# Forget-gate codes of a gated linear attention as plain fp32 products on four groups of array columns

## The chip, the cores and the metric

One core of one Trainium2 chip runs the whole program. The metric is the device time of one execution in microseconds; the kernel before took 2001.63 us as the median of three runs (1999.76 to 2003.19).

## The reference, cut to what matters

A sequence of 256 tokens with 1024 features passes through four layers: two of a first kind (feed-forward, a mixer, feed-forward) and two of a second kind, which the change does not touch. The mixer of the first kind runs a neighbourhood attention and a gated linear attention (GLA) side by side. The change concerns how GLA's two forget gates, one for each direction, are made from the normed input:

```python
h = rmsnorm(x, mix_norm)
proj = h @ w_in                     # [256,1024] @ [1024,3104]
na_q, na_k, na_v, g_q, g_k, g_v, g_r, gf_code, gb_code = jnp.split(proj, offsets, axis=-1)
...                                 # gf_code, gb_code: 16 columns each
log_gf = jax.nn.log_sigmoid((gf_code @ w_gate_f + b_gate_f).astype(f32)) / GLA_TAU
log_gb = jax.nn.log_sigmoid((gb_code @ w_gate_b + b_gate_b).astype(f32)) / GLA_TAU
...                                 # w_gate: [16,256]
o_fwd = gla_chunked(qg, kg, vg, log_gf, True)
o_bwd = flip(gla_chunked(flip(qg), flip(kg), flip(vg), flip(log_gb), False))
gla_o = rmsnorm(o_fwd + o_bwd, gla_gain).astype(x.dtype)
gla_o = merge_heads(gla_o) * jax.nn.silu(g_r)
x = x + jnp.concatenate([na_o, gla_o], axis=-1) @ w_out
```

Everything is fp32.

## The kernel before, in words

Features lie on the 128 partitions and tokens in the free dimension: `x` is 128 x 8 x 256 (eight blocks `kt` of 128 features). Most products keep fp32 accuracy with three passes in a fast format, fp32r: each weight block of 128 x 128 is split into a high part `wh` (ScalarE, L320) and a low part `wl` (VectorE, L333), the activations into `Hh` and `Hl`, and `mm3` (L617 on) issues `wh*Hh` (L621), `wh*Hl` (L622) and `wl*Hh` (L623), 256 columns each. The norm's token factor `rs` is not known when the products start; it is multiplied in when a tile leaves PSUM.

All large weights of the program come as one stream (class `Stream`): chunks of 16 weight blocks, 1 MB each, are loaded by SyncE's DMA queue into four staging buffers `stg`, split in two halves on ScalarE and VectorE up to two chunks ahead (`next`, `fill`, `prep`), and taken block by block by the products (`block`). The layout functions on the host (`lay_mix1`) set the order of the blocks.

`mix1` (L795 on) is the mixer of the first kind, run once in each of two layers. `tiles` gives a PSUM tile of two blocks of 128 outputs (count=1: one block), with 24 matmuls a block. Two tiles of it make g_r; then one block makes the codes: its weight block is 128 columns wide, of which columns 0 to 15 hold the forward code, 32 to 47 the backward code and the rest are zeros. Two VectorE products (L827) scale the 16 rows of each into the tile `code`, whose other rows were set to 1 by GpSimd (L804). Row 16 of each direction so carries a 1 that multiplies the bias, which `lay_gate` put into row 16 of `wgate`. Then `gla_gates` (L897 on) is started as a generator: it advances by one step at each `tick`, which `tiles` calls after every fourth step of its loop over `kt`. Its first step is four plain fp32 products (L903: two directions, two halves of 128 outputs) over 32 rows of the array, `zp = wgate * code`; then come the absolute value, the exponential and the logarithm on ScalarE (L909 to L912), the minimum and maximum on VectorE (L910), the difference (L914) and the running sums (L919). Meanwhile TensorE makes two tiles of GLA's keys and queries, two of the attention's values, four of its queries and keys (each followed by a softmax pair, `na_pair`, L1047 on), GLA's values, and the output product `mixed_out` (L869 on).

The mixer's stream has 17*8 + 2*32 + 64 = 264 blocks (`MIX1_BLOCKS`). That is 16.5 chunks, padded to 17; `mixed_out` ends with `st.skip()`, which drops the padding. With the codes' eight blocks in the third chunk, all later chunk boundaries fall into the middle of a tile.

The program's text is not the order of issue. A planner of the framework places each engine's instructions when the kernel is built: among those whose inputs and buffers are ready by its own cost estimates it takes the one that is needed first. An instruction written later can so be issued earlier on its engine; each engine then runs its list in that fixed order. PSUM and SBUF buffers under one tag are reused in turn, and a new user waits for the release of the old one. The lines that matter here, beside those in the listing:

```python
def mm3(self, out, w, kt, start, stop, clear=True):
    h, l = w
    ...
    mm(out[:, :n], h, self.Hh[:, kt, :n], ...)   # L621
    mm(out[:, :S], h, self.Hl[:, kt], ...)       # L622
    return mm(out[:, :n], l, self.Hh[:, kt, :n], ...)  # L623
```

One other place already uses plain fp32 products on four groups of 32 array columns: `compress` (L1427), in the last layer, with 16 products of 128 columns each, group after group:

```python
g = m % 4
nc.tensor.matmul(p[32 * g:32 * g + 32, :P], Z[j][:, m], w[:, m * P:(m + 1) * P], start=m < 4, stop=m >= 12)
```

Of the kernel before, what the change touches and what calls it, by code (L numbers as in the profile page):

```python
# [9 lines left out]
F32 = mybir.dt.float32  # L10
# [7 lines left out]
P = 128  # L18
S = 256
# [53 lines left out]
def lay_mix1(w_in, w_out):  # L73

    q, k, v, gq, gk, gv, gr, gf, gb = np.split(w_in, np.cumsum([512, 512, 512, 256, 256, 512, 512, 16]), 1)
    code = np.zeros((D, P), w_in.dtype)
    code[:, 0:RANK] = gf
    code[:, 32:32 + RANK] = gb
    q, k, gq, gk, gr, code, gv, v = [blocks(m) for m in (q, k, gq, gk, gr, code, gv, v)]
    seq = [gr, code]  # L80
    for i in range(2):
        seq += [gq[:, i], gk[:, i]]
    seq += token_blocks(v)
    for i in range(4):
        seq += [q[:, i], k[:, i]]
    wo = blocks(w_out)
    seq += token_blocks(gv) + [wo[:, :, :4], wo[:, :, 4:]]
    return cat(seq)


MIX1_BLOCKS = 17 * 8 + 2 * 32 + 64


def lay_rpb(rpb):
# [9 lines left out]
    return np.ascontiguousarray(b.reshape(2, P, 4 * 2 * S))  # L104


def lay_gate(wf, bf, wb, bb):

    o = np.zeros((64, 256), wf.dtype)
    for at, w, b in ((0, wf, bf), (32, wb, bb)):  # L110
        o[at:at + RANK] = w
        o[at + RANK] = b
    return o


def gla_masks():
# [21 lines left out]
def layout(i):  # L138
    o = {}
    for l in range(DEPTH):  # L140
        o[f"a1_{l}"] = lay_ffn(i["ffn1_wg"][l], i["ffn1_wu"][l], i["ffn1_wd"][l])
    o["xT"] = np.ascontiguousarray(i["x"][0].T.reshape(KD, P, S).transpose(1, 0, 2))
    for l in range(DEPTH):
        o[f"m1_{l}"] = lay_mix1(i["w_in"][l], i["w_out"][l])
        o[f"nab_{l}"] = lay_rpb(i["na_rpb"][l])
        o[f"wgate_{l}"] = lay_gate(i["w_gate_f"][l], i["b_gate_f"][l], i["w_gate_b"][l], i["b_gate_b"][l])
        o[f"a2_{l}"] = lay_ffn(i["ffn2_wg"][l], i["ffn2_wu"][l], i["ffn2_wd"][l])
    parts = []
    for l in range(DEPTH):
        parts += [(f"f1n{l}", i["ffn1_norm"][l]), (f"mxn{l}", i["mix_norm"][l]), (f"f2n{l}", i["ffn2_norm"][l]),  # L150
                  (f"nag{l}", i["na_gain"][l]), (f"glg{l}", i["gla_gain"][l])]
    parts += [("fin1", i["final_norm"]), ("fin2", i["final_norm_g_2"])]
    for l in range(DEPTH):
        mw = np.ascontiguousarray(i["mod_w_2"][l].T)
        o[f"mw_{l}"] = np.ascontiguousarray(mw.reshape(36, 2, P, D).transpose(0, 2, 1, 3).reshape(36, P, 2 * D))
        parts += [(f"mb{l}", i["mod_b_2"][l])] + [(f"ng{l}{j}", i["norm_g_2"][l, j]) for j in range(3)]
        w1 = i["ffn_w1_2"][l]
        for j in range(2):
            o[f"b{j}_{l}"] = lay_ffn(w1[j][:, :FF], w1[j][:, FF:], i["ffn_w2_2"][l, j])
    parts += [("cw", i["lru_conv_w_2"][0].reshape(-1)), ("cb", i["lru_conv_b_2"][0]),  # L160
              ("bab", np.concatenate([i["lru_ba_2"][0].reshape(-1), i["lru_bx_2"][0].reshape(-1)])),
              ("lam", i["lru_lambda_2"][0])]
    o["cond"] = np.ascontiguousarray(np.broadcast_to(i["c_2"], (P, D)))
    o["m2a"] = lay_mix2a(i["mix0_in_w_2"][0], i["mix0_out_w_2"][0])
    o["lru"] = lay_lru(i["lru_wa_2"][0], i["lru_wx_2"][0])
    o["m2b"] = lay_mix2b(i["mix1_in_w_2"][0], i["mix1_out_w_2"][0])
    o["cw1"] = np.ascontiguousarray(i["cmp_w1_2"][0].reshape(2, 16, P, P).transpose(0, 2, 1, 3).reshape(2, P, 2048))
    o["cpos"] = np.ascontiguousarray(i["cmp_pos_2"][0].reshape(2, 16, P).transpose(2, 0, 1))
    w2 = i["cmp_w2_2"][0]
    o["cw2"] = np.ascontiguousarray(np.concatenate([w2[0], w2[0], w2[1]], 1))  # L170
    o["rope"] = rope_tables()
    o["rot"] = rotation()
    o["causal"] = np.where(np.arange(P)[None] > np.arange(P)[:, None], np.float32(-1e30), np.float32(0))
    o["cmask"] = cmp_mask()
    o["masks"] = gla_masks()
    o["cols"] = lay_cols(parts)
    o["ident"] = np.eye(P, dtype=np.float32)
    return o
# [201 lines left out]
class Kern:  # L380
# [414 lines left out]
    def mix1(self, st, l, then):  # L795
        nc = self.nc
        with self.tc.tile_pool(name="mx", bufs=1) as mp, self.tc.tile_pool(name="m2", bufs=2) as m2, \
                self.phase_psum():
            self.bank, self.nst, self.pp = 256, 4, "pp"
            self.mp, self.m2 = mp, m2  # L800
            sgr = mp.tile([P, GH, S], F32, name="sgr")
            code = mp.tile([64, S], F32, name="code")
            wgate = mp.tile([64, S], F32, name="wgate")
            nc.gpsimd.memset(code, 1.0)  # L804
            nc.sync.dma_start(wgate, self.a[f"wgate_{l}"])
            kq = mp.tile([P, 2, 2, S], F32, name="kq")
            vg = mp.tile([P, 2, 512], F32, name="vg")
            vn = mp.tile([P, 2, 512], F32, name="vn")
            self.na = mp.tile([P, 4, S], F32, name="na")
            self.mh = mp.tile([P, 4, S], F32R, name="mh")  # L810
            self.ml = mp.tile([P, 4, S], F32R, name="ml")

            def scaled(p, w):
                t = m2.tile([P, 2, S], F32, name="t", tag="e0")
                nc.vector.tensor_tensor(t, p, self.rs2(), op=OP.mult)
                nc.scalar.activation(w, t, AF.Silu)

            p0 = self.tiles(st, first=True)

            def mid():  # L820
                scaled(p0, sgr[:, 0:2])

            p = self.tiles(st, mid=mid)
            scaled(p, sgr[:, 2:4])
            p = self.tiles(st, count=1)
            for at in (0, 32):
                nc.vector.tensor_mul(code[at:at + RANK], p[at:at + RANK, 0], self.rs[at:at + RANK])  # L827
            gates = self.gla_gates(l, code, wgate)
            self.bg.append(gates)
            if l == DEPTH - 1:  # L830
                self.small()
            for i in range(2):
                p = self.tiles(st)
                nc.vector.scalar_tensor_tensor(kq[:, 1, i], p[:, 0], 0.125, self.rs, op0=OP.mult, op1=OP.mult)
                nc.vector.tensor_mul(kq[:, 0, i], p[:, 1], self.rs)
            while gates in self.bg:
                self.tick()
            at = self.mp.tile([P, GH, 4, P], F32, name="at")

            def gla():  # L840
                yield from self.gla_grams(kq, at)
                yield
                yield from self.gla_out(l, at, vg, sgr)

            self.have_vg = self.pairs = 0
            self.bg.append(gla())
            for n in range(2):
                self.token_major(st, vn, n, 4)
            self.sqn, self.normed = None, False
            for i in range(4):  # L850
                p = self.tiles(st, ticks=1)
                qk = m2.tile([P, 2, S], F32, name="qk", tag="qk")
                nc.vector.scalar_tensor_tensor(qk[:, 0], p[:, 0], 0.125, self.rs, op0=OP.mult, op1=OP.mult)
                nc.vector.tensor_mul(qk[:, 1], p[:, 1], self.rs)
                if i % 2 == 0:
                    bias = st.raws.pop(0)
                self.bg.append(self.na_pair(l, i, qk, vn, bias))
            self.bg.append(self.na_norm())
            for n in range(2):
                self.token_major(st, vg, n, 1)  # L860
                self.have_vg = n + 1
            self.norm_start(*then())
            mm = nc.tensor.matmul

            while not self.normed:
                self.tick()
            self.mixed_out(st, (self.mh, self.ml), (self.gh, self.gl_))
# [29 lines left out]
    def gla_gates(self, l, code, wgate):  # L897
# [2 lines left out]
        zp = [self.pd.tile([P, 2, S], F32, name="zp", tag="pd") for _ in range(2)]  # L900
        for d in range(2):
            for i in range(2):
                nc.tensor.matmul(zp[d][:, i], wgate[32 * d:32 * d + 32, i * P:(i + 1) * P], code[32 * d:32 * d + 32],  # L903
                                 start=True, stop=True)
        yield
        az = mp.tile([P, 2, 2, S], F32, name="az")
        G = mp.tile([P, 2, 2, S], F32, name="G")
        for d in range(2):
            nc.scalar.activation(az[:, d], zp[d], AF.Abs)  # L909
            nc.vector.tensor_scalar(G[:, d], zp[d], 0.0, -288.0, op0=OP.min, op1=OP.max)  # L910
        nc.scalar.activation(az, az, AF.Exp, scale=-1.0)
        nc.scalar.activation(az, az, AF.Ln, bias=1.0)  # L912
        yield
        nc.vector.tensor_sub(G, G, az)  # L914
        self.INC = mp.tile([P, 2, 2, S], F32, name="INC")
        self.VAL = mp.tile([P, 2, 2, S], F32, name="VAL")
        for d in range(2):
# [767 lines left out]
```

## Time and profile before

| | before |
|---|---|
| median of three runs | 2001.63 us (1999.76 to 2003.19) |
| the profiled execution's own time | 2000.05 us |
| its span, first to last instruction | 1998.3 us |
| PE busy | 1962.8 us (98%), 13164 matmuls |
| DVE busy | 1592.4 us (80%) |
| ACT busy | 1179.2 us (59%) |
| POOL busy | 181.0 us (9%) |
| loaded | 430.92 MB, 216 GB/s in the mean |
[...]

PE is TensorE's matmuls, PEld its weight loads, DVE VectorE, ACT ScalarE, POOL GpSimd, SP SyncE with its DMA queue. Times in rows are microseconds from the start of the span unless marked ns. A matmul's duration includes the way through the array, so consecutive matmuls overlap: what one costs is read from the distance between two starts. A plain fp32 matmul appears as two instructions. The mixer of the first kind runs from about 195 to 327 us and from about 694 to 825 us.

### The profile page before, as it was taken

Reading aid. Unit: us, or ns where it says so; the run is one execution under the profiler, and the core shown is the slowest. Engines: PE = TensorE matmul, PEld = TensorE weight load, DVE = VectorE, ACT = ScalarE, POOL = GpSimd, SP = SyncE. Lnnn points to the kernel's source line nnn. Section 1 sums busy time; section 2 is a strip of 40 time slices with the busy share of each in tenths; the row PEclk is TensorE's granted clock in tenths of the full one; section 3 lists DMA queues with packets and bytes.
Section 4 is the critical chain, followed back from the end, with each engine's and each line's share of the span. In section 5 each row is a group of like instructions: output and inputs, shape, how many; then the busy total and the mean of one; then the engine's idle time right before and its main releaser. Section 6 shows DMA issues by size and latency. Waiting matters only on the chain.

```text
span 1998.3 us, 33132 instructions
## 1 busy us (share of the span) xinstructions
PE 1962.8 (98%) x13164; PEld 1779.0 (89%) x13164; DVE 1592.4 (80%) x2554; ACT 1179.2 (59%) x1977; POOL 181.0 (9%) x201
## 2 busy tenths in 40 slices
PE   8999999999999999999999999999999999999998
PEld 7888989888988898988898889898899888889887
DVE  8987888987888688898789878898667667988663
ACT  6654566554555566655556546675546655877652
POOL 3001002000100100200110010120010001111001
PEclk9999999999999999999999999999999999999999
DMA  7976434887687643488658864377555556315551
GB/s 293 326 280 237 173 136 172 297 295 264 230 290 273 238 177 135 177 297 291 257 194 294 295 246 162 126 260 278 190 190 189 190 190 200 108 50 195 190 185 56
DMA packets 67883, 430.92 MB, mean 216 GB/s; under 512 B 11408, under 2 KB 14096, under 8 KB 16656
## 3 DMA queue, kind: packets, MB, share of 16 engines
q1 hardware_dynamic: 67440, 428.28, 59.3%
q8 instruction: 103, 1.69, 0.3%
q10 hardware_dynamic: 288, 0.52, 0.1%
q14 instruction: 52, 0.43, 0.1%
HBM read 427.73 MB, written 1.05 MB: 215 GB/s over the span
## 4 chain that ended last, share of the span: by engine, by line
PE 88%; DVE 7%; ACT 3%; DMA 1%; issue 1%; POOL 0%; DVEq 0%; SPq 0%; ACTq 0%
PE pp L605 25%; PE pd L605 16%; PE pp L606 13%; PE pd L606 8%; PE pp L621 5%; PE pp L623 5%; PE pp L622 5%; PE po L883 2%; DVE wl L333 2%; PE pt L1275 1%; DVE Hl L686 1%; ACT wh L320 1%; PE pv L671 1%; PE pv L672 1%; PE pv L673 1%
## 5 line engine op out<-in xcount | busy, mean ns | idle before, releaser
L333 DVE TENSOR_TENSOR wl<-stg,wh 128x1024 fp32r<-128x1024 f32 x646 | 787.1, 1245 | 110.2 <-PE pd L606 44.8
L320 ACT ACTIVATE wh<-stg 128x1024 fp32r<-128x1024 f32 x646 | 667.4, 1053 | 299.4 <-PE pp L605 100.1
L605 PE MATMUL pp<-H,wh 128*128 128x512 f32 x2176 | 755.0, 390 | 0.0
L606 PE MATMUL pp<-H,wl 128*128 128x256 f32 x2176 | 613.6, 282 | 0.0
L605 PE MATMUL pd<-act,wh 128*128 128x512 f32 x1408 | 488.5, 390 | 0.0
L605 PEld LDWEIGHTS pp<-H,wh 128*128 128x128 f32 x2176 | 408.4, 188 | 85.8 <-DVE t L614 0.5
L606 PEld LDWEIGHTS pp<-H,wl 128*128 128x128 f32 x2176 | 411.2, 189 | 0.0
L606 PE MATMUL pd<-act,wl 128*128 128x256 f32 x1408 | 397.1, 282 | 0.0
L621 PE MATMUL pp<-Hh,wh 128*128 128x256 f32 (+1 forms) x1192 | 343.3, 288 | 7.6 <-ACT wh L291 6.8
L623 PE MATMUL pp<-Hh,wl 128*128 128x256 f32 (+1 forms) x1192 | 336.3, 282 | 1.2 <-DVE wl L333 1.0
L622 PE MATMUL pp<-Hl,wh 128*128 128x256 f32 x1192 | 334.9, 281 | 1.8 <-DVE Hl L686 1.8
L605 PEld LDWEIGHTS pd<-act,wh 128*128 128x128 f32 x1408 | 264.3, 188 | 55.4
L606 PEld LDWEIGHTS pd<-act,wl 128*128 128x128 f32 x1408 | 266.1, 189 | 0.0
L621 PEld LDWEIGHTS pp<-Hh,wh 128*128 128x128 f32 x1192 | 224.8, 189 | 12.3 <-ACT wh L291 6.8
L622 PEld LDWEIGHTS pp<-Hl,wh 128*128 128x128 f32 x1192 | 226.2, 190 | 3.9 <-DVE Hl L686 2.6
L623 PEld LDWEIGHTS pp<-Hh,wl 128*128 128x128 f32 x1192 | 225.1, 189 | 2.2 <-DVE wl L333 1.4
L700 DVE SCALAR_TENSOR_TENSOR stg<-stg,cond 128x1024 f32<-128x1024 f32 x144 | 176.2, 1226 | 35.1 <-DMA stg<-mw 32.0
L682 ACT ACTIVATE act<-a 128x256 fp32r<-128x256 f32 x176 | 73.4, 417 | 141.8 <-DVE a L758 129.4
L522 POOL TENSOR_TENSOR acc<-sq 128x256 f32<-128x256 f32 x16 | 17.3, 1081 | 1174.2 <-ACT sq L518 1174.1
L683 DVE TENSOR_TENSOR act<-a,act 128x256 fp32r<-128x256 f32 x176 | 76.4, 434 | 44.0 <-ACT act L682 44.0
L522 POOL TENSOR_TENSOR acc<-acc,sq 128x256 f32<-128x256 f32 x87 | 79.6, 918 | 330.3 <-ACT sq L518 326.6
L745 ACT ACTIVATE s<-t 128x256 f32<-128x256 f32 x136 | 56.6, 416 | 83.8 <-DVE t L614 83.3
(311 smaller groups left out, 2098.2 us busy)
## 6 DMA issues: line engine op xcount, KB each, us to landing
stg<-b SPq DMA_DIRECT2D x132, 1024.0 KB, 4.8
stg<-a SPq DMA_DIRECT2D x129, 1024.0 KB, 4.8
stg<-mw SPq DMA_DIRECT2D x72, 1024.0 KB, 5.8
stg<-m SPq DMA_DIRECT2D x34, 1024.0 KB, 4.8
stg<-m2a SPq DMA_DIRECT2D x14, 1024.0 KB, 4.8
stg<-m2b SPq DMA_DIRECT2D x12, 1024.0 KB, 5.0
stg<-nab SPq DMA_DIRECT2D x4, 1024.0 KB, 4.9
cond<-cond SPq DMA_DIRECT2D x6, 512.0 KB, 4.6
```

The lines of the kernel that those rows point to most:

```text
L320: self.k.nc.scalar.activation(h[:, sl], self.raw[c][:, sl], AF.Copy)
L333: self.k.nc.vector.tensor_sub(l[:, sl], t[:, sl], f(h[:, sl]))
L522: nc.gpsimd.tensor_tensor(s2, acc, sq, op=OP.add)
L605: mm(p, h, parts, start=start, stop=False)
L606: return mm(p[:, :S], l, parts[:, 1], start=False, stop=stop)
L621: mm(out[:, :n], h, self.Hh[:, kt, :n], start=start and clear, stop=False, skip_group_check=not clear)
L622: mm(out[:, :S], h, self.Hl[:, kt], start=False, stop=False, skip_group_check=not clear)
L623: return mm(out[:, :n], l, self.Hh[:, kt, :n], start=False, stop=stop, skip_group_check=not clear)
L682: nc.scalar.activation(hi, src, AF.Copy)
L683: nc.vector.tensor_sub(lo, src, f(hi))
L700: self.nc.vector.scalar_tensor_tensor(sl, sl, 1.0, self.cond, op0=OP.mult, op1=OP.mult, accum_out=self.mod[l][:, 2 * c + g:2 * c + g + 1])
L745: nc.scalar.activation(s, t[:, 0], AF.Silu)
```

## The change

The codes leave the weight stream. The 32 code columns come as a tensor of their own (`code_l`, 128 x 8 x 32, 128 KB), loaded at the start of the mixer and multiplied once by the norm's gain on VectorE. The products are plain fp32 on the unnormed, unsplit `x`: block `kt` goes to the group of 32 array columns `kt % 4`, so that four partial sums of the 32 code rows stand on the 128 partitions of one PSUM tile, each over two blocks. One VectorE product by `rs` takes all 128 rows into `code`. The gate weights are repeated four times along the 128 rows (`lay_gate`, 256 KB), with zeros for the other direction's rows, so that the gate products over 128 rows add the partial sums. The bias moves into ScalarE's and VectorE's instructions, which therefore work on one half of 128 outputs at a time; the lower limit moves into the difference. The stream has 256 blocks, which is 16 whole chunks.

```diff
 def lay_mix1(w_in, w_out):
-    code = np.zeros((D, P), w_in.dtype)
-    code[:, 0:RANK] = gf
-    code[:, 32:32 + RANK] = gb
-    q, k, gq, gk, gr, code, gv, v = [blocks(m) for m in (q, k, gq, gk, gr, code, gv, v)]
-    seq = [gr, code]
+    code = np.concatenate([gf, gb], 1).reshape(KD, P, 2 * RANK).transpose(1, 0, 2)
+    q, k, gq, gk, gr, gv, v = [blocks(m) for m in (q, k, gq, gk, gr, gv, v)]
+    seq = [gr]
...
-    return cat(seq)
-MIX1_BLOCKS = 17 * 8 + 2 * 32 + 64
+    return cat(seq), np.ascontiguousarray(code).reshape(P, -1)
+MIX1_BLOCKS = 16 * 8 + 2 * 32 + 64
...
-def lay_gate(wf, bf, wb, bb):
-    o = np.zeros((64, 256), wf.dtype)
-    for at, w, b in ((0, wf, bf), (32, wb, bb)):
-        o[at:at + RANK] = w
-        o[at + RANK] = b
-    return o
+def lay_gate(wf, wb):
+    o = np.zeros((4, 2 * RANK, 2, 256), wf.dtype)
+    o[:, :RANK, 0] = wf
+    o[:, RANK:, 1] = wb
+    return o.reshape(P, 512)
...
@@ mix1
-            code = mp.tile([64, S], F32, name="code")
-            wgate = mp.tile([64, S], F32, name="wgate")
-            nc.gpsimd.memset(code, 1.0)
-            nc.sync.dma_start(wgate, self.a[f"wgate_{l}"])
+            code = mp.tile([P, S], F32, name="code")
+            wgate = mp.tile([P, 2, S], F32, name="wgate")
+            nc.sync.dma_start(wgate, self.a[f"wgate_{l}"].rearrange("p (d n) -> p d n", d=2))
+            wcode = mp.tile([P, KD, 2 * RANK], F32, name="wcode")
+            nc.sync.dma_start(wcode, self.a[f"code_{l}"].rearrange("p (k n) -> p k n", k=KD))
...
-            p = self.tiles(st, count=1)
-            for at in (0, 32):
-                nc.vector.tensor_mul(code[at:at + RANK], p[at:at + RANK, 0], self.rs[at:at + RANK])
+            nc.vector.tensor_mul(wcode, wcode, self.g.unsqueeze(2).to_broadcast([P, KD, 2 * RANK]))
+            p = self.ps.tile([P, 2, S], F32, name="pco", tag="pp")
+            for kt in range(KD):
+                r = slice(32 * (kt % 4), 32 * (kt % 4) + 32)
+                nc.tensor.matmul(p[r, 0], wcode[:, kt], self.x[:, kt], start=kt < 4, stop=kt >= 4)
+            nc.vector.tensor_mul(code, p[:, 0], self.rs)
+            self.tick()
...
@@ gla_gates
-                nc.tensor.matmul(zp[d][:, i], wgate[32 * d:32 * d + 32, i * P:(i + 1) * P], code[32 * d:32 * d + 32],
-                                 start=True, stop=True)
+                nc.tensor.matmul(zp[d][:, i], wgate[:, d, i * P:(i + 1) * P], code, start=True, stop=True)
...
-            nc.scalar.activation(az[:, d], zp[d], AF.Abs)
-            nc.vector.tensor_scalar(G[:, d], zp[d], 0.0, -288.0, op0=OP.min, op1=OP.max)
+            for i in range(2):
+                b = self.col(f"bgate{l}", 2 * d + i)
+                nc.scalar.activation(az[:, d, i], zp[d][:, i], AF.Abs, bias=b)
+                nc.vector.tensor_scalar(G[:, d, i], zp[d][:, i], b, 0.0, op0=OP.add, op1=OP.min)
...
-        nc.vector.tensor_sub(G, G, az)
+        nc.vector.scalar_tensor_tensor(G, G, -288.0, az, op0=OP.max, op1=OP.subtract)
```

The host also adds the four bias columns of each layer to the small table `cols`.

## Rows read from the trace of the kernel before

**Rows 1.** The page's chain that ended last: share of the span by engine.

```profile
PE 88%; DVE 7%; ACT 3%; DMA 1%; issue 1%; POOL 0%; DVEq 0%; SPq 0%; ACTq 0%
```

**Rows 2.** Busy us (x instructions) by stretch: PE, PEld, DVE, ACT, POOL; clock, DMA, GB/s.

```profile
225.00:285.00 60.00, 56.81 (x496) 51.05 (x495) 56.28 (x98) 36.06 (x73) 0.87 (x1) 1.00 0.45 160
724.00:784.00 60.00, 57.07 (x497) 51.16 (x497) 56.22 (x98) 36.43 (x73) 0.87 (x1) 1.00 0.45 163
```

**Rows 3.** Waits of PE, 195 to 335 us: us in total, times, longest.

```profile
PE pav L1089 <- ACT pt L1082: 1.9, 1, 1.9
PE pss L1054 <- DVE qk L854: 0.9, 2, 0.7
PE pp L622 <- DVE Hl L686: 0.5, 1, 0.5
```

**Rows 4.** Timeline of PE around the codes, layer 0: start, duration, engine, line, operation.

```profile
207.38 0.28 PE L621 MATMUL pp<-Hh,wh 128*128 128x256 f32 x1
...
210.21 0.28 PE L621 MATMUL pp<-Hh,wh 128*128 128x256 f32 x1
...
211.51 0.28 PE L623 MATMUL pp<-Hh,wl 128*128 128x256 f32 x1
211.72 1.14 PE L903 MATMUL zp<-code,wgate 32*128 32x256 f32 x8
212.79 0.38 PE L621 MATMUL pp<-Hh,wh 128*128 128x256 f32 x1
213.01 0.28 PE L622 MATMUL pp<-Hl,wh 128*128 128x256 f32 x1
```

**Rows 5.** Timeline of `compress`: plain fp32 on four column groups, and what follows.

```profile
1689.31 0.84 PEld L1427 LDWEIGHTS pq<-stg,Z 128*32 128x32 f32 x32 [0.96 <-issue]
1689.34 1.08 PE L1427 MATMUL pq<-stg,Z 128*32 128x128 f32 x32 [0.78 <-issue]
...
1690.35 0.39 PE L621 MATMUL pp<-Hh,wh 128*128 128x258 f32 x1
...
1690.57 0.28 PE L622 MATMUL pp<-Hl,wh 128*128 128x256 f32 x1
```

**Rows 6.** All of line L1427: durations in ns, minimum/median/maximum.

```profile
L1427 PEld LDWEIGHTS pq<-stg,Z x64: 106/110/110, 1689.3 to 1694.0; 128*32 128x32 f32 x64
```

**Rows 7.** Timeline of PE: plain fp32 over 128 rows and 128 columns (L1212).

```profile
1221.23 1.02 PE L1212 MATMUL pl<-xc,wlru 128*128 128x256 f32 x4
...
1222.21 0.28 PE L622 MATMUL pp<-Hl,wh 128*128 128x256 f32 x1
```

**Rows 8.** Timeline of DVE around the codes, layer 0.

```profile
207.58 0.69 DVE L815 TENSOR_TENSOR t<-pp,rs 128x512 f32<-128x512 f32 x1 [1.72 <-PE pp L623]
208.19 2.35 DVE L333 TENSOR_TENSOR wl<-stg,wh 128x1024 fp32r<-128x1024 f32 x2
210.48 0.86 DVE L827 TENSOR_TENSOR code<-pp,rs 16x256 f32<-16x256 f32 x2
213.51 1.29 DVE L910 TENSOR_SCALAR G<-zp 128x512 f32<-128x512 f32 x2 [2.18 <-ACT az L909]
```

**Rows 9.** Timeline of DVE in layer 1: the first and last of 27 small ones (`small`, written after the codes).

```profile
697.93 0.16 DVE L433 TENSOR_SCALAR sp<-lam 128x4 f32<-128x4 f32 x1
...
706.52 0.17 DVE L436 TENSOR_SCALAR ns<-ns 128x4 f32<-128x4 f32 x1
```

**Rows 10.** The page's DVE group that splits weights, and its DMA issues.

```profile
L333 DVE TENSOR_TENSOR wl<-stg,wh 128x1024 fp32r<-128x1024 f32 x646 | 787.1, 1245 | 110.2 <-PE pd L606 44.8
...
stg<-m SPq DMA_DIRECT2D x34, 1024.0 KB, 4.8
```

**Rows 11.** Issue of the table of masks on SyncE, and median landing of a 256 KB load.

```profile
196.12 0.58 SPq L926 DMA_DIRECT2D masks<-masks  x1
...
rope<-rope SPq DMA_DIRECT2D x2, 256.0 KB, 3.6
```

**Rows 12.** Timeline of ACT at the gates' first step, layer 0.

```profile
212.88 1.08 ACT L909 ACTIVATE az<-zp 128x512 f32<-128x512 f32 x2 [2.85 <-PE zp L903]
```

More of the change, by code (lines that the diff above doesn't have):

```diff
@@ L143, in layout @@
     for l in range(DEPTH):
-        o[f"m1_{l}"] = lay_mix1(i["w_in"][l], i["w_out"][l])
+        o[f"m1_{l}"], o[f"code_{l}"] = lay_mix1(i["w_in"][l], i["w_out"][l])
         o[f"nab_{l}"] = lay_rpb(i["na_rpb"][l])
-        o[f"wgate_{l}"] = lay_gate(i["w_gate_f"][l], i["b_gate_f"][l], i["w_gate_b"][l], i["b_gate_b"][l])
+        o[f"wgate_{l}"] = lay_gate(i["w_gate_f"][l], i["w_gate_b"][l])
         o[f"a2_{l}"] = lay_ffn(i["ffn2_wg"][l], i["ffn2_wu"][l], i["ffn2_wd"][l])
@@ L150, in layout @@
         parts += [(f"f1n{l}", i["ffn1_norm"][l]), (f"mxn{l}", i["mix_norm"][l]), (f"f2n{l}", i["ffn2_norm"][l]),
-                  (f"nag{l}", i["na_gain"][l]), (f"glg{l}", i["gla_gain"][l])]
+                  (f"nag{l}", i["na_gain"][l]), (f"glg{l}", i["gla_gain"][l]),
+                  (f"bgate{l}", np.concatenate([i["b_gate_f"][l], i["b_gate_b"][l]]))]
     parts += [("fin1", i["final_norm"]), ("fin2", i["final_norm_g_2"])]
```

## The prediction

> **What bounds the kernel now.** I read the page first. Its chain of waits lies on TensorE for 88% of the span and on VectorE for 7% [rows 1], so a change is worth what it takes off TensorE's list, unless TensorE stands waiting where the change works. The busy times by stretch say where it does: in the 60 us of each mixer that hold the attention's softmax and GLA's gram products, VectorE is busy for 56.28 and 56.22 us and TensorE for only 56.81 and 57.07 [rows 2]. So the mixer has two regimes: around the codes (205 to 225 us) TensorE runs without a gap, and from 225 to 285 us VectorE's list sets the pace and TensorE loses about 3 us. The waits name the places: 1.9 us for the transposed softmax weights, 0.9 us for an eviction of queries and keys, 0.5 us for the low part of the normed input at the mixer's end [rows 3]. Last I read the timelines around the codes for the prices.
>
> **The change part by part, for one layer; there are two.**
>
> *The codes' products leave the three-pass stream.* Their 24 matmuls run from 207.38 us to the start of the next tile at 210.21 us: 2.83 us, 0.118 us each [rows 4]. All of it is TensorE's own time, with nothing beside it that has to wait: minus 2.83 us.
>
> *Plain fp32 products on four column groups come in.* Eight products are 16 instructions of 256 columns, 4096 columns in all. The nearest rows are those of `compress`, which has the same form on the same four groups: 32 instructions of 128 columns, also 4096. They go from 1689.34 us to the next start at 1690.35 us, 1.01 us, and the matmul after that start takes 0.22 us to its successor instead of 0.12, so 0.10 us more [rows 5]. What the switch into a tiled array costs shows at the gate products, which start 0.21 us after the matmul before them instead of 0.12: 0.09 us [rows 4]. I take 1.01 + 0.10 + 0.09 = 1.20 us. Below it stands perfect concurrency: plain fp32 over the full array costs 0.215 us per instruction of 256 columns (four of them from 1221.23 us to 1222.21 less one step of 0.12, so 0.86 us [rows 7]), and four to a group make 0.86 us. Above it stands no concurrency, 16 x 0.215 + 0.19 = 3.63 us. I take the middle value because the row has the same form, and only the columns per instruction differ.
>
> *The weight loads of the small blocks.* There are 16, of 32 columns. In `compress` 32 such loads last about 0.110 us each [rows 6], 3.5 us one after another, and yet all lie within 0.84 us [rows 5]; they overlap, and 1.20 us holds them. [...]
>
> *The gate products go from 32 rows to 128.* Before, two directions stand on two row groups and partly overlap: from 211.63 us (211.51 plus a step) to 212.89 us (213.01 less a step), 1.26 us with both switches [rows 4]. After, eight instructions use the whole array: 8 x 0.215 = 1.72 us [rows 7]. Plus 0.46 us; the two ends, 0.36 and 0.56, differ only by whether a switch remains.
>
> TensorE's sum: -2.83 + 1.20 + 0.46 = -1.17 us per layer, -2.34 us for both.
>
> *The code weights times the gain, on VectorE.* This is new: 256 columns on 128 partitions, at 0.43 us as the code evictions (0.86 us for two of 256 columns [rows 8]). Its inputs are early: the table of masks, written far behind, is issued at 196.12 us, and 256 KB take 3.6 us to land [rows 11], so both new loads are there by about 201 us. The codes start at 207.38 us. VectorE sits idle for 1.72 us before 207.58 us [rows 8], and in layer 1 the planner put 27 small instructions, written after the codes, into just such gaps from 697.93 us on [rows 9]. So I cost it at nothing. If the planner puts it where it is written, it stands behind the eviction of g_r's second tile (207.58 + 0.69 us), ends at 208.70 us, and TensorE waits 1.2 us from 207.50; that is the second rival.
>
> *The code eviction* is one instruction instead of two (minus 0.43 us of VectorE). Behind it in the list come the low halves of the next chunk (2.35 us [rows 8]), needed only after a whole tile, 16 x 3 x 0.118 = 5.7 us later. The gate products come twelve matmuls, 1.41 us, after the code products; an eviction of 0.43 us fits, and behind one half split (1.2 us) it would be late by 0.2 us. I cost that at nothing.
>
> *The gates' first step in quarters.* VectorE's two minima of 512 columns (1.29 us [rows 8]) become four of 256, at 0.43 us 1.72: plus 0.43 us. ScalarE's two absolute values (1.08 us [rows 12]) become four, between 1.08 and 2.16 us. Neither is on TensorE's path; TensorE reaches the gate products 1.63 us earlier and leaves them 1.17 us earlier, so the gates' chain begins earlier by as much as TensorE does, and the VectorE-bound stretch moves with it.
>
> *One chunk less in the stream.* 34 loads of 1 MB become 32 [rows 10]; two halves of the low split go, 2 x 1.245 = 2.49 us of VectorE per layer [rows 10], and two of the high split on ScalarE. New loads of 0.38 MB take the place of 0.064 MB. DMA is busy for 0.45 of the stretch [rows 2], so the bytes count nothing. VectorE's net is -2.49 + 0.43 - 0.43 + 0.43 = -2.06 us. Where TensorE is the bound this is worth nothing. In the VectorE-bound stretch it is worth something, but only half a chunk falls there: each boundary moves from the middle of a tile to its start, so a low half is due half a tile later, 1.25 us of VectorE less before the attention's end, against a TensorE loss of 3.19 us (60 - 56.81 [rows 2]). Bounds: all TensorE waits but the eviction's go (-1.8 us, the 1.9 us of the pair less a remnant), or the splits now fall on the softmax (third rival). I take -0.4 us, a third of 1.25, since the waits hang on latencies more than on the sum: -0.8 us for both layers.
>
> **Sum.** -2.34 - 0.8 = -3.1 us. The profiled execution took 2000.05 us around a span of 1998.3 us; it would take 1996.9 us. It lies 1.58 us under the median of the runs, 2001.63 us; so I forecast 1998.5 us.
>
> **Rivals.**
>
> First, *VectorE's relief is cashed in full.* For it: the 3 us lost per layer [rows 2, 3], and 2.06 us less work. Against: the wait of 1.9 us ends on a chain of softmax, transpose and copy that the change does not shorten. Then -2.34 - 2 x 1.8 = -5.9 us: 1995.7 us.
>
> Second, *the small weights are scaled too late.* For it: the text has the scaling behind the eviction. Against: [rows 9]. Two waits of 1.25 us: -2.34 + 2.5 = +0.2 us: 2001.8 us.
>
> Third, on the other side, *the splits land on the softmax.* With boundaries at tile starts, the next chunk's splits ask for VectorE just when a tile's eviction and its softmax pair do, and TensorE waits for a low half. The place is the four tiles of queries and keys; the price one half, 1.245 us, each: 4 x 1.245 - 1.17 = +3.8 us per layer, 2009.2 us. It makes the kernel slower than 0.2% from three of the four boundaries on. For it: VectorE is busy for 94% there [rows 2]. Against: splits run up to two chunks ahead, and no row of the waits names `wl` [rows 3].
>
> Fourth, *the small loads are paid one after another*: 16 x 0.110 + 0.86 + 0.19 = 2.81 us instead of 1.20, so +0.44 us per layer: 2002.5 us. [...] Against: [rows 5].
>
> Fifth, *the four groups do not overlap*, so the change does not do what it says: 3.63 us, +1.26 us per layer: 2004.2 us.
>
> **How the numbers follow.** The forecast has 0.55, with a range of its own from 1996.0 to 2001.0 us; the rivals in order 0.22, 0.08, 0.09, 0.04, 0.02. Two tenths of a per cent, 4.0 us, is about what a measurement of this kernel can tell from no change: faster is below 1997.6 us, slower above 2005.6 us. The forecast gives 0.15 to faster, the first rival 0.20: 0.35. Slower takes 0.09 of the third and 0.01 of others: 0.10. The rest, 0.55, is same. The range 1993.5 to 2004.5 us reaches over all but the third rival.
>
> **What would show it.** The distance from the last matmul of g_r's second tile to the first of the next tile should be about 1.3 us instead of 2.83 + 0.12; with a gap before the small products, the second rival holds; with more than 2.5 us and no gap, the fourth or fifth. The gate products should take 1.72 us. `stg<-m` should count 32, L333's group 642. In the stretch with the softmax, TensorE's waits for `pt`, `qk` and any new one for `wl` decide between the forecast, the first and the third. A time above 2003 us with both small terms as priced would make the prediction wrong in its second part; elsewhere, outside both mixers, the order of issue should leave the times as they are.

## The result and the profile after

The changed kernel takes 2014.17 us, the median of six runs (2009.86 to 2015.45), against 2001.45 us (1999.76 to 2003.19) for the kernel before beside it: a ratio of 1.0058, 95% interval 1.0048 to 1.0068, estimated from all runs and so not exactly the quotient of the medians. By the medians it is 12.7 us slower. The forecast was 1998.5 us, in a range up to 2004.5 us, so the prediction was wrong. The profiled execution took 2014.43 us around a span of 2012.4 us, 14.1 us more than before's, at a mean granted clock of 0.996 of TensorE's full speed (before: 0.998).

The page first: the busy times, the chain by engine (before: [rows 1]), the splits and the stream's issues (before: [rows 10]).

```profile
PE 1980.5 (98%) x13148; PEld 1778.4 (88%) x13148; DVE 1589.5 (79%) x2554; ACT 1177.4 (59%) x1977; POOL 181.8 (9%) x199
...
PE 88%; DVE 7%; ACT 2%; issue 1%; DMA 1%; POOL 1%; DVEq 0%; SPq 0%; ACTq 0%; POOLq 0%
...
L331 DVE TENSOR_TENSOR wl<-stg,wh 128x1024 fp32r<-128x1024 f32 x642 | 782.2, 1245 | 138.5 <-PE pp L604 58.5
...
stg<-m SPq DMA_DIRECT2D x32, 1024.0 KB, 4.8
```

The work left out is as the prediction counted it: 32 loads of the stream instead of 34, 642 halves of the split instead of 646. TensorE has 16 matmuls fewer and is yet busy for 17.7 us more (1962.8 before). VectorE and ScalarE have less to do. So TensorE's time must have grown where the change took nothing away.

The timeline of TensorE around the codes, layer 0, answers [rows 4].

```profile
209.81 0.28 PE L621 MATMUL pp<-Hh,wl 128*128 128x256 f32 x1
210.03 1.07 PE L829 MATMUL pco<-x,wcode 128*32 128x256 f32 x16
211.03 0.39 PE L619 MATMUL pp<-Hh,wh 128*128 128x256 f32 x1
211.25 0.28 PE L620 MATMUL pp<-Hl,wh 128*128 128x256 f32 x1
...
212.54 1.89 PE L907 MATMUL zp<-code,wgate 128*128 128x256 f32 x8
214.08 0.47 PE L619 MATMUL pp<-Hh,wh 128*128 128x256 f32 x1
214.39 0.28 PE L620 MATMUL pp<-Hl,wh 128*128 128x256 f32 x1
```

From 209.93 us (209.81 plus a step of 0.118) to 211.13 us (211.25 less a step) the code products cost 1.20 us with both switches; 2.83 us before. From 212.54 to 214.27 us (214.39 less a step) the gate products cost 1.73 us; 1.26 before. No gap lies ahead of either. In layer 1 the gate products cost 1.73 us as well, but the code products 1.51: they are over so soon that TensorE then stands for 0.25 us, at 714.97 us, until VectorE has evicted the second tile of g_r (L814).

The timeline of VectorE there answers [rows 8].

```profile
201.96 0.41 DVE L825 TENSOR_TENSOR wcode<-wcode,cols 128x256 f32<-128x256 f32 x1
...
210.13 0.69 DVE L814 TENSOR_TENSOR t<-pp,rs 128x512 f32<-128x512 f32 x1 [1.69 <-PE pp L621]
...
211.87 0.42 DVE L830 TENSOR_TENSOR code<-pco,rs 128x256 f32<-128x256 f32 x1
```

The scaling of the small weights stands 8 us before its products, and VectorE is idle for 1.4 us behind it. The eviction of the codes ends at 212.29 us, before the gate products at 212.54.

Busy us by stretch in both mixers, the 60 us that answer to [rows 2], and 3.4 us inside the first (columns as there: the last three are granted clock, DMA share and GB/s).

```profile
226.40:286.40 60.00, 57.73 (x493) 52.09 (x492) 55.66 (x99) 36.48 (x73) 1.46 (x2) 0.97 0.49 176
730.60:790.60 60.00, 57.70 (x491) 52.09 (x490) 55.62 (x99) 36.47 (x73) 1.47 (x2) 0.97 0.49 176
...
274.40:277.80 3.40, 3.40 (x16) 2.69 (x14) 3.40 (x8) 1.32 (x6) 0.00 (x0) 0.50 0.83 306
```

And the waits of TensorE, 195 to 335 us, which answer to [rows 3].

```profile
PE pss L1059 <- ACT sq L516: 1.7, 1, 1.7
PE pss L1059 <- DVE qk L858: 0.6, 1, 0.6
PE pgr L542 <- POOL rcol L536: 0.6, 1, 0.6
PE pbc L542 <- POOL rcol L536: 0.5, 1, 0.5
```

TensorE stands waiting for 2.27 and 2.30 us instead of 3.19 and 2.93: a gain of 0.9 and 0.6 us. The wait for `qk` was there before, the wait of 1.9 us for `pt` is gone, and one of 1.7 us for a square on ScalarE (`sq`) is new. It ends at 273.62 us, and from 274.4 us on the clock is granted at 0.50 for 3.4 us. From that I estimate 1.7 us of work lost, half of 3.4.

None of this makes 12 us. The first matmul of the first mixer starts later than before already; before and after:

```profile
195.36 0.28 PE L621 MATMUL pp<-Hh,wh 128*128 128x256 f32 x1
...
197.93 0.28 PE L619 MATMUL pp<-Hh,wh 128*128 128x256 f32 x1
```

So 2.6 us are gone ahead of the mixer, in a feed-forward layer that the change does not touch: TensorE's first 1244 matmul instructions, up to the codes' products, are the same in the same order. From there to the first pair of matmuls (below) behind the mixer, 158.93 us became 158.00, and in layer 1 158.88 became 158.80. The loss lies in the feed-forward layers. One of them by windows, before:

```profile
360.00:420.00 60.00, 60.00 (x348) 53.20 (x347) 53.61 (x78) 36.28 (x55) 0.00 (x0) 1.00 0.78 283
```

and the same stretch after, with one of a later layer:

```profile
360.00:420.00 60.00, 60.00 (x341) 52.27 (x340) 51.62 (x76) 35.02 (x54) 0.00 (x0) 1.00 0.81 295
1060.00:1120.00 60.00, 60.00 (x346) 52.55 (x345) 54.23 (x80) 36.23 (x55) 0.00 (x0) 1.00 0.85 303
```

TensorE is busy without a gap (60.00 of 60 us) at the full clock (1.00) in all three, and does 348 matmuls in the one and 341 or 346 in the others. So it is neither a wait nor the clock. The matmuls come in pairs, one of 512 columns with the high half `wh` and one of 256 with the low half `wl` (L605 and L606 before, L603 and L604 after). The timeline of a few, before and then after:

```profile
99.93 0.39 PE L605 MATMUL pp<-H,wh 128*128 128x512 f32 x1
...
101.32 0.39 PE L605 MATMUL pp<-H,wh 128*128 128x512 f32 x1
...
99.71 0.39 PE L603 MATMUL pp<-H,wh 128*128 128x512 f32 x1
99.94 0.28 PE L604 MATMUL pp<-H,wl 128*128 128x256 f32 x1
...
101.47 0.40 PE L603 MATMUL pp<-H,wh 128*128 128x512 f32 x1
```

Before, the four pairs from 99.93 to 101.32 us take 1.39 us, 347 ns each; after, the five from 99.71 to 101.47 take 1.76 us, 352 ns each. Over all pairs the mean distance from one pair's start to the next is 346.7 ns before, in every layer. After, it is 353.4 ns in the first four and the last of the eight feed-forward blocks and 348.9 ns in the other three, 351.7 ns in the mean. There are 3584 pairs: 3584 x 5.0 ns = 17.9 us.

What differs for these pairs is where their operands lie. The change adds four bias columns per layer to `cols`, which grows from 298 to 306 columns, 32 bytes per partition. All that was allocated behind it moved by 32 bytes: `act` from 145824 to 145856, `H` from 190880 and 194976 to 190912 and 195008. The weights `wh` and `wl` lie ahead of `cols` and stayed, at addresses that 128 divides. `act` and `H` are what streams through the pairs. Take the remainder of each address by 128 bytes: the streamed operand stood 32 bytes from the weights before, and stands 64 bytes from them after.

### The profile page after: what moved, and what is told of

The parts are those of the page before. It is cut to its first block, busy times and chain, and to the rows that moved or that the text cites. A ratio compares the mean times of both kernels' runs of the same rounds, so it can differ in the third digit from the quotient of the medians.

```text
span 2012.4 us, 33077 instructions
## 1 busy us (share of the span) xinstructions
PE 1980.5 (98%) x13148; PEld 1778.4 (88%) x13148; DVE 1589.5 (79%) x2554; ACT 1177.4 (59%) x1977; POOL 181.8 (9%) x199
## 4 chain that ended last, share of the span: by engine, by line
PE 88%; DVE 7%; ACT 2%; issue 1%; DMA 1%; POOL 1%; DVEq 0%; SPq 0%; ACTq 0%; POOLq 0%
PE pp L603 25%; PE pd L603 16%; PE pp L604 13%; PE pd L604 8%; PE pp L619 5%; PE pp L621 5%; PE pp L620 5%; PE po L887 3%; DVE wl L331 3%; PE pt L1280 1%; DMA stg<-a 1%; ACT wh L318 0%; PE pav L1575 0%; PE pv L669 0%; DVE e L1066 0%
## 5 line engine op out<-in xcount | busy, mean ns | idle before, releaser
L603 PE MATMUL pp<-H,wh 128*128 128x512 f32 x2176 | 765.6, 395 | 0.0
L604 PE MATMUL pp<-H,wl 128*128 128x256 f32 x2176 | 612.2, 281 | 0.0
L603 PE MATMUL pd<-act,wh 128*128 128x512 f32 x1408 | 495.5, 395 | 0.0
L603 PEld LDWEIGHTS pp<-H,wh 128*128 128x128 f32 x2176 | 409.1, 188 | 96.9
L604 PEld LDWEIGHTS pp<-H,wl 128*128 128x128 f32 x2176 | 408.2, 188 | 0.1
L604 PE MATMUL pd<-act,wl 128*128 128x256 f32 x1408 | 396.1, 281 | 0.0
L621 PE MATMUL pp<-Hh,wl 128*128 128x256 f32 (+1 forms) x1176 | 332.2, 283 | 1.0 <-DVE wl L331 1.0
L620 PE MATMUL pp<-Hl,wh 128*128 128x256 f32 x1176 | 330.5, 281 | 0.8 <-DVE Hl L684 0.8
L603 PEld LDWEIGHTS pd<-act,wh 128*128 128x128 f32 x1408 | 264.7, 188 | 62.9
L604 PEld LDWEIGHTS pd<-act,wl 128*128 128x128 f32 x1408 | 264.1, 188 | 0.0
L520 POOL TENSOR_TENSOR acc<-sq 128x256 f32<-128x256 f32 x16 | 17.9, 1124 | 1184.4 <-ACT sq L516 1173.6
L612 DVE TENSOR_TENSOR t<-pp,c 128x512 f32<-128x512 f32 x136 | 93.0, 684 | 1.3 <-ACT c L610 0.5
```

Source lines behind the costliest of these rows:

```text
L520: nc.gpsimd.tensor_tensor(s2, acc, sq, op=OP.add)
L603: mm(p, h, parts, start=start, stop=False)
L604: return mm(p[:, :S], l, parts[:, 1], start=False, stop=stop)
L612: self.nc.vector.tensor_tensor(t, p[:, :, S:], c, op=OP.add)
L620: mm(out[:, :S], h, self.Hl[:, kt], start=False, stop=False, skip_group_check=not clear)
L621: return mm(out[:, :n], l, self.Hh[:, kt, :n], start=False, stop=stop, skip_group_check=not clear)
```

## The experiments

The theory is called A in the expectations, where it stands in the form that it had at the time: the place of the streamed operand against the weights sets the time of a pair, and what the change was meant to do is worth its 3 us. The rivals: the changed instructions and their order slow the rest (contention from other loads, other clock), or any shift of the whole layout does. "place" is the distance of `act` and `H` from the weights in bytes, as a remainder by 128; "pair" is the mean over all pairs of a profile. Medians compare with runs of the kernel before on the same chip: 2004.03 us for e1 to e4, 2002.84 for e5 to e8, 2002.39 for e9 to e12.

| kernel | place | pair, ns | median, us | ratio to before, 95% |
|---|---|---|---|---|
| before | 32 | 346.7 | | |
| after | 64 | 351.7 | 2014.17 | 1.0058 [1.0048, 1.0068] |
| e1_after_cols8 | 96 | 350.0 | 2010.71 | 1.0035 [1.0022, 1.0048] |
| e2_before_cols8 | 64 | 351.1 | 2017.39 | 1.0074 [1.0058, 1.0091] |
| e3_before_cols16 | 96 | 350.0 | 2015.69 | 1.0063 [1.0048, 1.0078] |
| e4_before_h8 | `H` 64, `act` 32 | 351.3, 346.7 | 2013.68 | 1.0054 [1.0039, 1.0069] |
| e5_after_bias_own | 32 | 346.7 | 1998.91 | 0.9982 [0.9973, 0.9991] |
| e6_before_cols32 | 32 | 346.7 | 2004.54 | 1.0002 [0.9993, 1.0011] |
| e7_before_cols24 | 0 | 351.1 | 2018.21 | 1.0070 [1.0054, 1.0085] |
| e8_before_all8 | 32 | 346.7 | 2003.09 | 0.9998 [0.9989, 1.0007] |
| e9_before_w8 | 0 | 351.1 | 2020.63 | 1.0089 [1.0075, 1.0103] |
| e10_before_off48 | 48 | 350.0, 349.6 | 2012.84 | 1.0054 [1.0038, 1.0071] |
| e11_before_off16 | 16 | 346.7 | 2005.32 | 1.0019 [1.0008, 1.0030] |
| e12_after_cols24 | 32 | 346.7 | 1999.47 | 0.9980 [0.9970, 0.9990] |

Where two pair times stand, the first is that of the pairs with `H`, the second of those with `act`. In all nine variants of the kernel before, TensorE's matmuls stand in that kernel's order, and in the three of the kernel after in its order.

**Padding of the table (e1, e2, e3).** The kernel after with 8 columns more, and the kernel before with 8 and with 16:

```diff
-        self.cols = cp.tile([P, ncol], F32, name="cols")
+        self.cols = cp.tile([P, ncol + 8], F32, name="cols")[:, :ncol]
```

> The changed kernel with the table of columns widened by 8 unused columns, so that everything placed behind it in SBUF moves by 32 more bytes (act from byte 145856 to 145888); order and waits of every engine stay. Theory A, the place of the moving operand: the wide feed-forward matmuls step 228 + 118 ns again, eight feed-forward layers lose nothing, about 17.6 us come back: 2014.2 - 17.6 = 1996.6 us. Rival B, the cause is in the mixers or in the order of issue: 2014 us as before.

> The kernel before, with the table of columns widened by 8 unused columns, so that act lies at byte 145856 as in the changed kernel; nothing else. Theory A: the feed-forward pairs of matmuls take 349 to 353 ns instead of 346.7, 8 to 24 us more, likeliest 17.6: 2019 us. Rival B: 2001.5 us.

> The kernel before, widened by 16 unused columns: act at 145888. Theory A as the remainder of the address by 64 bytes (32 here and in the kernel before, 0 in the changed one): 2001.5 us, 346.7 ns a pair. Rival A2, another part of the address counts (by 128 bytes, or one absolute place): slower than 2001.5 us by 5 to 18.

e2 is the kernel before with 32 unused bytes, and it is slower than the changed kernel. Its window:

```profile
360.00:420.00 60.00, 60.00 (x341) 52.33 (x340) 52.57 (x77) 35.47 (x54) 0.00 (x0) 1.00 0.82 295
```

341 matmuls, as in the kernel after, without any of the change. Its pairs explain it: 3584 x 4.4 ns = 15.8 us, measured 13.4. e1 and e3 missed: both stand at 96, 64 bytes on from before's 32, and the old rhythm did not come back (350.0 ns in both), so the place does not count by 64 bytes.

**One operand alone (e4).** Eight unused elements behind `act` move `H`, and the small tiles behind it, and leave `act`:

```diff
-            act = ap.tile([P, NF, 2, S], F32R, name="act")
+            act = ap.tile([P, NF * 2 * S + 8], F32R, name="act")[:, :NF * 2 * S]
+            act = act.rearrange("p (f d s) -> p f d s", f=NF, d=2)
```

> The kernel before, with 32 unused bytes behind act in the feed-forward layers: act stays at 145824, H (moving operand of the first half) goes from 190880 and 194976 to 32 bytes more, and so do the small tiles behind it. Theory A, the moving operand's place: the pairs of the first half (pp<-H, 272 a layer) slow to 349 to 353 ns, those of the second half (pd<-act, 176 a layer) stay at 346.7; 61% of 17.6 us: 2012 us. Rival A3, it is some other tile behind the table of columns: both halves alike.

Its two groups of 512 columns (instructions, busy us, mean ns):

```profile
L605 PE MATMUL pp<-H,wh 128*128 128x512 f32 x2176 | 765.1, 395 | 0.1
...
L605 PE MATMUL pd<-act,wh 128*128 128x512 f32 x1408 | 488.5, 390 | 0.0
```

Those that stream `H` last 395 ns, as in the kernel after; those that stream `act` last 390 ns, as before. 2176 x 4.6 ns = 10.0 us, measured 9.7. One execution holds both rhythms, at a granted clock of 1.00 in both (360 to 420 and 460 to 500 us), and the order and the loads are before's. TensorE's pairs read none of the small tiles that moved along.

**The biases kept elsewhere (e5).** The changed kernel with the bias columns behind the code weights in their own tile, so that `cols` has 298 columns again:

```diff
-            wcode = mp.tile([P, KD, 2 * RANK], F32, name="wcode")
+            wc = mp.tile([P, KD * 2 * RANK + 4], F32, name="wcode")
...
-                b = self.col(f"bgate{l}", 2 * d + i)
+                b = self.bgate[:, 2 * d + i:2 * d + i + 1]
```

> The changed kernel with the four bias columns of a layer kept behind the code weights in the mixer's own tile, so that the table of columns has its old width and act and H lie where the kernel before has them (145824; 190880 and 194976). The mixers are those of the change. Theory A (the place of act and H carries the loss): every feed-forward pair at 346.7 ns, the changed kernel's 2014.2 less 18.0 us (5 layers x 448 pairs x 6.7 ns and 3 x 448 x 2.2 ns in its trace) is 1996 us, 5 us under the kernel before. Rival C (the mixers lose as well, by TensorE's clock at its lower level there): 2000 us or more.

Its window:

```profile
360.00:420.00 60.00, 60.00 (x348) 53.20 (x347) 52.16 (x78) 36.18 (x55) 0.00 (x0) 1.00 0.81 291
```

All the work of the change is there, the pairs are back at 346.7 ns, and it is faster than before by 3.9 us.

**Period and reference (e6, e7, e8, e9).** e6 and e7 pad `cols` of the kernel before by 32 and by 24 columns. e8 puts 32 unused bytes ahead of everything; e9 puts them ahead of `wh` and `wl` and pads `cols` by 24, so that weights and streamed operands stand at the same remainder. The lines of e9 (e8 has the same tile ahead of the staging buffers):

```diff
+        front = ctx.enter_context(tc.tile_pool(name="front", bufs=1)).tile([P, 8], F32, name="front")
+        nc.gpsimd.memset(front, 0.0)
```

> The kernel before, table of columns widened by 32 unused columns: act at 145952, 128 bytes on. If the place counts by its remainder by 128 bytes (32 in the kernel before; 64 and 96 were slow): 346.7 ns a pair and 2002 us. If it counts by a larger remainder or the absolute place: 349 to 353 ns and 8 to 18 us more.

> The kernel before, widened by 24 unused columns: act at 145920, remainder 0 by 128 bytes, the one not tried. If only the remainder 32 is fast: 349 to 353 ns, 2010 to 2020 us. If remainder 0 is fast as well, or faster: 346.7 ns or less, 2002 us or less.

> The kernel before with 32 unused bytes ahead of everything in SBUF: weights (wh, wl), x, Hh, Hl, act and H all move by 32 bytes together; act lies at 145856 as in the changed kernel. If the absolute place of the moving operand counts: 349 to 353 ns, about 2017 us, as the kernel before widened by 8 columns. If its place against the weights' counts: 346.7 ns, 2002 us.

> The kernel before with 32 unused bytes ahead of the split weights (wh, wl) and the table of columns widened by 24: weights at remainder 32 by 128 bytes instead of 0, act and H at 145952 and their like, remainder 32 as in the kernel before; the staging buffers stay. If the place of act and H against the weights counts (now 0, as with 24 columns alone): 351.1 ns a pair, 2018 us. If their place against anything else, or for itself: 346.7 ns, 2003 us.

128 bytes more (e6, 346.7 ns) are as none; 96 (e7, 351.1 ns) are slow. In e8 `act` stands at 145856, the address that is slow in e2 and after, and the pairs take 346.7 ns, since the weights moved too. Its window:

```profile
360.00:420.00 60.00, 60.00 (x348) 53.20 (x347) 53.62 (x78) 36.11 (x55) 0.00 (x0) 1.00 0.80 283
```

In e9 `act` and `H` keep the remainder 32 that is fast before, the weights move to it, and the pairs are slow, 351.1 ns:

```profile
360.00:420.00 60.00, 60.00 (x343) 52.57 (x343) 52.71 (x77) 34.75 (x55) 0.00 (x0) 1.00 0.81 294
```

So in these runs it is the distance between the two operands that counts, by 128 bytes, and no address by itself (346.7 ns at 32 in before, e6 and e8, 351.1 at 0 in e7 and e9); e9 also excludes the distance from the staging buffers, which did not move and from which `act` and `H` stand, by 128, as before.

**Steps of 16 bytes (e10, e11).** `act` and `H` begin 16 bytes into their tiles, in e11 with `cols` padded by 24 as well; for `H`:

```diff
-        self.H = pool.tile([P, KD, 2, S], F32R, name="H")
+        H = pool.tile([P, KD * 2 * S + 8], F32R, name="H")[:, 4:4 + KD * 2 * S]
```

> The kernel before with act and H begun 16 bytes into their tiles: remainder 48 by 128 against the weights' 0. Theory A has no price for it: places tried so far gave 351.1 (0), 346.7 (32), 351 to 352 (64) and 350.0 ns (96). If the fast place is a stretch of 32 bytes from 32 on: 346.7 ns, 2003 us; if it is the one place: 348 to 352 ns, 2007 to 2020 us.

> The kernel before, table widened by 24 columns, act and H begun 16 bytes into their tiles: remainder 16 by 128. If whole steps of 32 bytes count: 351.1 ns as at 0, 2018 us; if it lies between its neighbours: 346.7 to 351, 2003 to 2018 us.

16 is as fast as 32 (346.7 ns). 48 is slow but for one group: the pairs of e10 with `act` take 346.7 ns in the first feed-forward block and 350.0 in the other seven. e11's time does not follow its pairs: at 346.7 ns it is 0.19% over before, with runs from 2001.8 to 2010.8 us (before, on that chip: 1999.9 to 2010.5). Its profiled execution took 2002.03 us, 2.0 more than before's, and those lie in the second mixer, where the clock fell to 0.50 for 3.4 us (from 780.3 us). What made its longer runs is not explained.

**The change at the old place (e12).** The changed kernel with `cols` padded by 24, in the one line of e1.

> The changed kernel whole, with one line altered: the table of columns widened by 24 unused columns, so that act and H come to remainder 32 by 128 bytes again (act 145952). Theory A, as a remainder by 128: 346.7 ns a pair, and the time of the changed kernel with its bias columns elsewhere, 1999 us, 0.2% under the kernel before. If it was the removal of the bias columns from the table that helped: 2010 to 2014 us.

The pairs are at 346.7 ns and the time is 1999.47 us, 0.998 of before [0.997, 0.999]; e12 and e5 beat both kernels. By stage, in e12's profile against before's, the mixers gain 0.67 and 0.60 us, and another 1.27 us lie between 1008 and 1040 us, where the kernel's second kind of layer begins. (e5's profile shows no such gain: its mixers take 0.69 and 0.28 us more than before's. That execution took 2002.18 us, near the longest of e5's ten, and in its mixers the clock stood at 0.50 for 6.8 and 3.4 us.) Between 1008 and 1040 us one wait of TensorE is shorter; before:

```profile
PE pbc L544 <- DVE rc L557: 2.6, 1, 2.6
```

and e12:

```profile
PE pbc L542 <- DVE rc L555: 1.4, 1, 1.4
```

It belongs to the change: the same wait is 2.4 to 3.0 us in all ten profiles without it and 1.2 to 1.9 us in all four with it. Why VectorE reaches that reciprocal earlier was not tried.

## Why the prediction was wrong

The step that failed is the last one: "elsewhere, outside both mixers, the order of issue should leave the times as they are". The order did, but for about 1 us saved where the second kind begins; the layout did not. The prediction counted instructions, loads and waits, and gave the bias columns in `cols` no cost, not even a place in the sum; they shifted the operands of 3584 pairs by 32 bytes, which costs 17.9 us. No rival had it: all five priced the mixer. By the shift alone (e2) the kernel before becomes slower by 13.4 us, and without the shift (e5, e12) the change is faster by 3.9 and 2.9 us. That the place is the cause is shown (`act` at 145856: 351.1 ns a pair in e2, and 346.7 in e8, where the weights moved along); through what it acts no run here shows.

The terms of the sum, in the prediction's order:

- *Code products*: 1.20 us forecast, 1.20 measured in layer 0 and 1.51 in layer 1, where the sum had no term for the wait of 0.25 us behind them. `compress` was the right row. The products start four at a time, 0.22 us apart, which is what one instruction over the full array costs (0.215): the four groups run side by side in full, and the rest of the 1.20 us lies at the ends: 0.09 us ahead of the first four, 0.11 us behind the last four and 0.10 us behind the next tile's first matmul. The lower end of 0.86 us left that out. The fourth and fifth rivals, 2.81 and 3.63 us, are out. The 16 small loads, 106 to 110 ns each, lie within 0.59 us while the products run.
- *Gate products*: 1.72 us forecast, 1.73 measured.
- *Scaling of the weights*: nothing forecast, nothing measured; the planner hoisted it. The second rival is out.
- *Code eviction and the gates' quarters*: no wait of TensorE names them. Right.
- *VectorE's relief*: 0.4 us per layer forecast; the waits of the stretch shrank by 0.9 and 0.6 us, more than forecast and less than the first rival's 1.8. The prediction let the wait for `pt` stand; it went, and one nearly as long (1.7 us, on ScalarE) came elsewhere.
- *What came back*: the prediction had no term for the clock. Behind the new wait it falls for 3.4 us in each mixer, which by the estimate above gives back some 1.7 us. In e12 it falls too:

```profile
272.40:275.80 3.40, 3.40 (x24) 3.18 (x24) 3.28 (x8) 2.03 (x9) 0.00 (x0) 0.50 0.84 292
```

  All 14 profiles together show what this costs; a mixer is counted from its first matmul to the first pair behind it. Of the 20 mixers without the change, 15 have no fall and take 159.0 us in the mean (158.7 to 159.5), and five have one and take 160.7 (160.2 to 161.1). All eight with the change have one; seven, with a fall of 3.4 us, take 158.5 us in the mean (158.0 to 159.2), and one of e5, with 6.8 us, takes 159.6. So against a mixer with a fall the change gains some 2.1 us, more than the 1.57 forecast; but the fall is there in all eight with the change, and against a mixer without one about 0.5 us are left.
- *The third rival*, the only one beyond the range on the slower side: no wait of TensorE names `wl`. The time came out slower for another reason.
- *The sum*: -3.1 us forecast. At the old place -2.9 us (e12: 1999.47 against 2002.39) and -3.9 us (e5). The size agrees, but its parts do not: about 1 us of it lies in the two mixers, where 3.1 were forecast, and another 1.27 us (e12) where the second kind begins, which the prediction put at nothing. The agreement is luck in good part.

The prediction's own test pointed the right way: "a time above 2003 us with both small terms as priced" was said to make it wrong in its second part. Both terms are as priced, and the time is above; but the second part was not to blame.

## What to carry to other kernels

Here 32 bytes more in one long-lived tile, `cols`, moved every tile behind it, so print the addresses before and after, and look at the distance between two starts of a matmul that the change does not touch. If that distance differs in a stretch where TensorE has no gap at the full clock (here 346.7 against 351.7 ns a pair), compare where its two operands lie before looking for a wait. Padding one tile (here by 96 bytes) is a cheap control: it separates what an edit does from what its layout does.

## What was not expected of the hardware

A pair of a 512- and a 256-column matmul on fp32r operands took 346.7 ns with the streamed operand 16 or 32 bytes from the weights by 128, and 349.6 to 351.7 ns in a profile's mean at 0, 48, 64 and 96: 0.8 to 1.4% of a pair, and up to 18 us of this kernel. The place does not settle the rhythm alone. At 64 two rhythms stand side by side, 353.4 and 348.9 ns in different layers of one run at the same addresses; the last block has the first of them in the kernel after and the second in e2; e4 has a third, 350.2 ns, in its first block; and at 48 one group of e10 keeps 346.7. What chooses between them stays open.

So does what makes the clock fall. In the stretch of the softmax it fell in both mixers of all four profiles with the change (after, e1, e5, e12). Of the ten without it, it fell in one mixer in five (e4, e6, e7, e9, e11) and in none in five (before, e2, e3, e8, e10).
